# Rotary embedding on one core: the two head rows loaded as two transfers, one ahead of cosine, one behind sine

## The chip, the cores and the metric

The kernel runs on one core of one Trainium2 chip. The metric is the device time of one execution in microseconds (us). The kernel before took 316.34 us, the median of 3 runs (316.33 to 316.51).

## What is computed

The input x has 8 batches of 2048 positions, 16 heads and 64 values per head, in float32. Each head's 64 values are taken as two halves, which are rotated by the angle of their position:

```python
x1 = x[..., :32]; x2 = x[..., 32:]
cos = cos[None, :, None, :]; sin = sin[None, :, None, :]
out1 = x1 * cos - x2 * sin
out2 = x1 * sin + x2 * cos
return concatenate([out1, out2], axis=-1)
```

x and the output have 67.1 MB each; cosine and sine have 2048 x 32 values each, 256 KB.

## The kernel before

**Tiling.** Of a batch's 2048 positions each of the 128 partitions holds 16 consecutive ones (J = 16), called rows here. A row is 16 heads of 64 values (W = 1024 values, 4 KB in float32), and over all partitions one row of a batch is 512 KB. Work in SBUF is in 16-bit floats: `buf` has five slots of one batch each (SLOTS = 5), and batch b lives in slot b mod 5.

**Queues.** Nearly all of x goes through POOL's DMA queue, q0 in the profile, which turns float32 into float16 on the way in and back on the way out. The helper `queue` (lines 56 to 66) fixes the order in which these transfers are issued to the order of the calls in the program; I call it the ring. Two helpers issue on it: `load` (line 72) and `store` (line 75). Their records all stand at line 57. ScalarE's queue (q10) and SyncE's queue (q1) carry plain float32 transfers: sine on SyncE's (line 50), and cosine and then the head on ScalarE's (lines 51 and 52).

**The head.** The first two rows of batch 0 (JA = 2) do not come through the ring. They are loaded as float32 into `head` (line 44), which is the space of the first rows of slot 4 seen as 32-bit words, and ScalarE narrows them into slot 0 with `narrow_head` (line 95, the copy is line 96), first row 0 (JF = 1) and then row 1. The other 14 rows of batch 0 are the first load of the ring, load(0), at line 100. Since slot 4 holds the head until ScalarE has read it, load(3,2), the load of batches 3 and 4, has to wait for both `narrow_head` calls.

**Tables.** ScalarE also narrows the tables: sine twice into `sin_h` (line 101, and with the sign turned at line 102), and cosine once into `cos_h` (line 103). ScalarE runs its instructions in the order of the program.

**Rotation.** `rotate` (line 78) makes three VectorE instructions for some rows of one batch: the product of the swapped halves with sine into `v` (line 87), the product with cosine in place (line 91), and their sum in place (line 93).

**Order of the work.** The program's tail calls, in this order: load(0); the table copies and the two narrowings; rotate row 0 of batch 0; store of row 0 (512 KB of output); load(1,2), that is batches 1 and 2; load(3,2); rotate rows 1 to 15 of batch 0 and store them; rotate 1 and 2, and store both; and so on to batch 7. The last two rows of batch 7 are widened by ScalarE (line 127) and go out on SyncE's queue (line 128) when the first nine rows of batch 7 have been written.

So the order of the ring is: load(0), store of row 0, load(1,2), load(3,2), store of rows 1 to 15, store(1,2), load(5), load(6,2), store(3,2), store(5,2), and two stores of batch 7. POOL issues each of them only when what it needs is there, and those behind it wait on POOL.

Of the kernel before, what the change touches and what calls it, by code (L numbers as in the profile page):

```python
# [1 line left out]

# [4 lines left out]


@with_exitstack  # L10
def kernel(
    ctx: ExitStack,
    tc: tile.TileContext,
    x: bass.AP,
    cos: bass.AP,
    sin: bass.AP,
    out: bass.AP,
):
    nc = tc.nc
    f16 = mybir.dt.float16  # L20
    f32 = mybir.dt.float32

    B, S, H, D = x.shape
    Dh = D // 2
    P = nc.NUM_PARTITIONS
    J = S // P
    SLOTS = 5
    JA = 2
    JE = 2
    JF = 1  # L30

    pool = ctx.enter_context(tc.tile_pool(name="rope", bufs=1))
    buf = pool.tile([P, SLOTS, J, H, D], f16)
    v = pool.tile([P, J, H, D], f16)
    sin_f = pool.tile([P, J, Dh], f32)
    cos_f = pool.tile([P, J, Dh], f32)
    cos_h = pool.tile([P, J, Dh], f16)
    sin_h = pool.tile([P, J, D], f16)

    def words(slot, rows):  # L40
        flat = buf[:, slot, 0 : 2 * rows].rearrange("p j h d -> p (j h d)")
        return flat.bitcast(f32)

    head = words(SLOTS - 1, JA)
    tail = words(SLOTS - 2, JE)
    rows_in = x.rearrange("b (p j) h d -> p b (j h d)", j=J)
    rows_out = out.rearrange("b (p j) h d -> p b (j h d)", j=J)
    W = H * D

    nc.sync.dma_start(out=sin_f, in_=sin.rearrange("(p j) d -> p j d", j=J))  # L50
    nc.scalar.dma_start(out=cos_f, in_=cos.rearrange("(p j) d -> p j d", j=J))  # L51
    nc.scalar.dma_start(out=head, in_=rows_in[:, 0, 0 : JA * W])

    ring = []

    def queue(dst, src):
        dma = nc.gpsimd.dma_start(out=dst, in_=src)  # L57
        if ring:
            tc.add_manual_dep(
                dma.ins,  # L60
                ring[-1].ins.name,
                mybir.DependencyInfo(mybir.DependencyClass.NoSync, mybir.DependencyReason.DATA),
                reason="order of the ring",
            )
        ring.append(dma)
        return dma

    def part(b, n, j0, j1):
        s = b % SLOTS
        return buf[:, s : s + n, j0:j1].rearrange("p n j h d -> p n (j h d)")  # L70

    def load(b, n=1, j0=0):
        return queue(part(b, n, j0, J), rows_in[:, b : b + n, j0 * W : J * W])

    def store(b, n=1, j0=0, j1=J):
        return queue(rows_out[:, b : b + n, j0 * W : j1 * W], part(b, n, j0, j1))

    def rotate(b, j0=0, j1=J):
        n = j1 - j0
        js = slice(j0, j1)  # L80
        xt = buf[:, b % SLOTS, js]
        vt = v[:, js]
        shape = [P, n, H, 2, Dh]
        sin_b = sin_h[:, js, :].rearrange("p j (e d) -> p j e d", e=2).unsqueeze(2).to_broadcast(shape)
        cos_b = cos_h[:, js, :].unsqueeze(2).to_broadcast([P, n, 2 * H, Dh])
        xe = xt.rearrange("p j h (e d) -> p j h e d", e=2)
        nc.vector.tensor_mul(  # L87
            out=vt.rearrange("p j h (e d) -> p j h e d", e=2), in0=xe[:, :, :, ::-1, :], in1=sin_b
        )
        xw = xt.rearrange("p j h (e d) -> p j (h e) d", d=Dh)  # L90
        nc.vector.tensor_mul(out=xw, in0=xw, in1=cos_b)  # L91
        xa = xt.rearrange("p j h d -> p (j h d)")
        nc.vector.tensor_add(out=xa, in0=xa, in1=vt.rearrange("p j h d -> p (j h d)"))  # L93

    def narrow_head(j0, j1):
        nc.scalar.copy(  # L96
            out=buf[:, 0, j0:j1].rearrange("p j h d -> p (j h d)"), in_=head[:, j0 * W : j1 * W]
        )

    load(0, j0=JA)  # L100
    nc.scalar.copy(out=sin_h[:, :, Dh:D], in_=sin_f)  # L101
    nc.scalar.mul(out=sin_h[:, :, 0:Dh], in_=sin_f, mul=-1.0)  # L102
    nc.scalar.copy(out=cos_h, in_=cos_f)  # L103
    narrow_head(0, JF)
    narrow_head(JF, JA)
    rotate(0, 0, JF)
    store(0, j1=JF)
    load(1, 2)
    load(3, 2)
    rotate(0, JF, J)  # L110
    store(0, j0=JF)
    rotate(1)
    rotate(2)
    store(1, 2)
    load(5)
    load(6, 2)
    rotate(3)
    rotate(4)
    store(3, 2)
    rotate(5)  # L120
    rotate(6)
    store(5, 2)
    rotate(7)
    gate = store(7, j1=9)
    store(7, j0=9, j1=J - JE)

    nc.scalar.copy(out=tail, in_=buf[:, (B - 1) % SLOTS, J - JE : J].rearrange("p j h d -> p (j h d)"))  # L127
    end = nc.sync.dma_start(out=rows_out[:, B - 1, (J - JE) * W : J * W], in_=tail)
    tc.add_manual_dep(
        end.ins,  # L130
        gate.ins.name,
        mybir.DependencyInfo(mybir.DependencyClass.Sync, mybir.DependencyReason.DATA),
        reason="the last rows go out behind this part",
    )


# [1 line left out]
_INS = ['x', 'cos', 'sin']  # L138
_OUTS = [((8, 2048, 16, 64), 'float32')]


# [23 lines left out]
```

## Time and profile before

One execution was profiled. Its own time is 316.32 us, and its span from the first to the last instruction is 314.6 us.

| What | Value |
|---|---|
| Median of 3 runs | 316.34 us |
| Profiled execution / its span | 316.32 us / 314.6 us |
| VectorE busy, 27 instructions | 209.1 us |
| ScalarE busy, 7 instructions | 6.8 us |
| POOL's DMA queue q0, share of the 16 DMA engines | 98.1% |
| SyncE's queue q1 / ScalarE's queue q10 | 1.2% / 1.0% |
| HBM read and written | 67.63 MB and 67.11 MB |
| Issue to landing: sine / cosine / head | 3.7 / 3.9 / 12.1 us |
| Issue to landing: load(0) / store of row 0 | 22.6 / 8.4 us |

How to read the profile: DVE is VectorE, ACT is ScalarE, POOL is GpSimd and SP is SyncE. A line such as "L91 DVE TENSOR_TENSOR buf<-buf,cos_h" is an instruction of program line 91 that writes `buf` from `buf` and `cos_h`; what stands in brackets behind it is how long its engine was idle before it and what ended the wait. Line 57 stands for every transfer of the ring. The view by stretches gives, for each stretch of the span, the busy time of each engine and what share of the 16 DMA engines was busy with packets; a packet is counted with its whole length in the stretch where it starts, so short stretches can show shares over one, and long ones can be over or under by a little. A transfer is cut into packets: each of the 16 engines gets eight data packets of a 128-partition transfer and one small one that reports the completion.

### The profile page before, as it was taken

The numbers are of one execution on the slowest core, as the hardware profiler recorded it, in microseconds if no ns is written. First come the engines' busy times: TensorE is split into PE (matmuls) and PEld (weight loads), VectorE is DVE, ScalarE is ACT, GpSimd is POOL, SyncE is SP. The second block draws the span as 40 slices with busy tenths as digits, with TensorE's granted clock in tenths as the row PEclk, the third lists the DMA queues.
The fourth block names the chain that finished last, engine by engine and source line by source line (L and its number), as shares of the span: only waits on it lengthen the run. The fifth ranks groups of instructions, "written<-read, shape, count | busy, mean of one in ns | idle before, by whom it ended". The sixth has DMA issues, their size and how long they took to land.

```text
span 314.6 us, 113 instructions
## 1 busy us (share of the span) xinstructions
DVE 209.1 (66%) x27; ACT 6.8 (2%) x7; POOL 7.9 (3%) x16
## 2 busy tenths in 40 slices
DVE  0109991089999999999994399903999999200000
ACT  3200000000000000000000000000000000200000
POOL 1020000000000000000000000000000000100000
DMA  7989999999999899999999999999999999999998
GB/s 230 261 193 249 267 200 200 200 267 200 200 200 325 375 500 400 400 400 533 400 200 221 246 200 200 250 217 333 400 517 417 400 400 525 408 400 400 433 425 342
DMA packets 3072, 101.71 MB, mean 323 GB/s; under 512 B 256, under 2 KB 256, under 8 KB 640
## 3 DMA queue, kind: packets, MB, share of 16 engines
q0 software_dynamic: 2496, 99.09, 98.1%
q1 hardware_dynamic: 288, 1.31, 1.2%
q10 hardware_dynamic: 288, 1.31, 1.0%
HBM read 67.63 MB, written 67.11 MB: 428 GB/s over the span
## 4 chain that ended last, share of the span: by engine, by line
DVE 59%; DMA 19%; another core or an unknown queue 7%; ACT 1%; issue 0%; POOL 0%; ACTq 0%; DVEq 0%
DVE v L87 20%; DVE buf L91 20%; DVE buf L93 20%; DMA buf<-in_x_dram 19%; ACT buf L127 1%; ACT buf L96 0%; POOL out_dram L57 0%; ACTq L51 0%; DVEq L87 0%
## 5 line engine op out<-in xcount | busy, mean ns | idle before, releaser
L87 DVE TENSOR_TENSOR v<-buf,sin_h 128x16384 f16<-128x16384 f16 (+2 forms) x9 | 69.7, 7744 | 59.7 <-DMA buf<-in_x_dram 45.3
L91 DVE TENSOR_TENSOR buf<-buf,cos_h 128x16384 f16<-128x16384 f16 (+2 forms) x9 | 69.7, 7744 | 0.3
L93 DVE TENSOR_TENSOR buf<-buf,v 128x16384 f16<-128x16384 f16 (+2 forms) x9 | 69.7, 7744 | 0.3
L57 POOL DMA_DIRECT2D out_dram<-buf x7 | 4.3, 620 | 219.7 <-DVE buf L93 219.7
L127 ACT CAST buf<-buf 128x2048 f32<-128x2048 f16 x1 | 1.9, 1897 | 254.2 <-DVE buf L93 254.2
L57 POOL DMA_DIRECT2D buf<-in_x_dram x5 | 3.4, 679 | 43.0 <-DMA out_dram<-buf 42.2
L96 ACT CAST buf<-buf 128x1024 f16<-128x1024 f32 x2 | 2.0, 1042 | 7.2 <-DMA buf<-in_x_dram 7.2
L101 ACT ACT_TABLE_LOAD x1 | 1.3, 1283 | 1.7 <-PEq L149 1.7
L101 ACT CAST sin_h<-sin_f 128x512 f16<-128x512 f32 x1 | 0.6, 617 | 1.5 <-DMA sin_f<-in_sin_dram 1.5
L102 ACT ACTIVATE sin_h<-sin_f 128x512 f16<-128x512 f32 x1 | 0.6, 624 | 0.0
L103 ACT CAST cos_h<-cos_f 128x512 f16<-128x512 f32 x1 | 0.6, 601 | 0.0
L149 POOL MEMSET const-float32-0.0<- 128x1 f32 x1 | 0.1, 99 | 0.2 <-issue 0.2
L149 POOL MEMSET const-bfloat16-1.0<- 128x1 bf16 x1 | 0.1, 102 | 0.0
L149 POOL MEMSET const-float32-1.0<- 128x1 f32 x1 | 0.1, 99 | 0.0
L149 POOL MEMSET const-uint8-127<- 128x1 uint8 x1 | 0.1, 99 | 0.0
## 6 DMA issues: line engine op xcount, KB each, us to landing
buf<-in_x_dram POOLq DMA_DIRECT2D x3, 8192.0 KB, 57.1
out_dram<-buf POOLq DMA_DIRECT2D x1, 7680.0 KB, 71.7
out_dram<-buf POOLq DMA_DIRECT2D x1, 4608.0 KB, 35.5
buf<-in_x_dram POOLq DMA_DIRECT2D x1, 4096.0 KB, 57.3
buf<-in_x_dram POOLq DMA_DIRECT2D x1, 3584.0 KB, 22.6
out_dram<-buf POOLq DMA_DIRECT2D x1, 2560.0 KB, 41.0
buf<-in_x_dram ACTq DMA_DIRECT2D x1, 1024.0 KB, 12.1
out_dram<-buf SPq DMA_DIRECT2D x1, 1024.0 KB, 8.4
```

The lines of the kernel that those rows point to most:

```text
L57: dma = nc.gpsimd.dma_start(out=dst, in_=src)
L87: nc.vector.tensor_mul(out=vt.rearrange("p j h (e d) -> p j h e d", e=2), in0=xe[:, :, :, ::-1, :], in1=sin_b)
L91: nc.vector.tensor_mul(out=xw, in0=xw, in1=cos_b)
L93: nc.vector.tensor_add(out=xa, in0=xa, in1=vt.rearrange("p j h d -> p (j h d)"))
L96: nc.scalar.copy(out=buf[:, 0, j0:j1].rearrange("p j h d -> p (j h d)"), in_=head[:, j0 * W : j1 * W])
L101: nc.scalar.copy(out=sin_h[:, :, Dh:D], in_=sin_f)
L102: nc.scalar.mul(out=sin_h[:, :, 0:Dh], in_=sin_f, mul=-1.0)
L103: nc.scalar.copy(out=cos_h, in_=cos_f)
L127: nc.scalar.copy(out=tail, in_=buf[:, (B - 1) % SLOTS, J - JE : J].rearrange("p j h d -> p (j h d)"))
L149: nc = _bacc.Bacc("TRN2", target_bir_lowering=False, num_devices=1)
```

## The change

Three lines at the top and one in the order of the narrowings are touched.

```diff
     nc.sync.dma_start(out=sin_f, in_=sin.rearrange("(p j) d -> p j d", j=J))
+    nc.scalar.dma_start(out=head[:, 0:W], in_=rows_in[:, 0, 0:W])
+    nc.sync.dma_start(out=head[:, W : JA * W], in_=rows_in[:, 0, W : JA * W])
     nc.scalar.dma_start(out=cos_f, in_=cos.rearrange("(p j) d -> p j d", j=J))
-    nc.scalar.dma_start(out=head, in_=rows_in[:, 0, 0 : JA * W])
...
     nc.scalar.copy(out=sin_h[:, :, Dh:D], in_=sin_f)
     nc.scalar.mul(out=sin_h[:, :, 0:Dh], in_=sin_f, mul=-1.0)
+    narrow_head(0, JF)
     nc.scalar.copy(out=cos_h, in_=cos_f)
-    narrow_head(0, JF)
     narrow_head(JF, JA)
```

The head's one transfer of 1 MB becomes two of 512 KB. ScalarE's queue carries row 0 and then cosine; SyncE's queue carries sine and then row 1. On ScalarE the narrowing of row 0 goes ahead of that of cosine. The ring, the rotations and the stores are the same.

## The prediction

> **What bounds the kernel now.** I read the page first. VectorE is busy 66% of the span and the three other engines hardly at all, but the slices of the DMA engines stay at 8 or 9 tenths, and POOL's queue alone fills them.
>
> ```profile
> span 314.6 us, 113 instructions
> DVE 209.1 (66%) x27; ACT 6.8 (2%) x7; POOL 7.9 (3%) x16
> DMA  7989999999999899999999999999999999999998
> q0 software_dynamic: 2496, 99.09, 98.1%
> ```
>
> The slices are coarse, so I then cut the span into stretches at the points where POOL's transfers end (columns: stretch, length, busy times of DVE, ACT and POOL, PE clock, share of the 16 DMA engines, GB/s).
>
> ```profile
> 2.60:23.24 20.64, 2.07 (x3) 3.98 (x6) 1.95 (x3) 1.00 1.01 252
> 23.24:24.46 1.22, 0.52 (x1) 0.00 (x0) 0.00 (x0) 1.00 1.22 416
> 24.46:63.11 38.65, 23.95 (x3) 0.00 (x0) 0.55 (x1) 1.00 1.01 217
> 101.74:119.83 18.09, 18.02 (x3) 0.00 (x0) 0.71 (x1) 1.00 1.02 435
> 158.44:310.55 152.11, 88.24 (x11) 1.90 (x1) 3.25 (x5) 1.00 1.01 352
> ```
>
> In every stretch the share is one or a little over (a packet is counted where it starts): from about 2.6 us to the last transfer there is no gap on the engines. I checked this in the trace's packet records, where each packet of an engine starts as the one before ends. So the chain of waits, which names VectorE with 59%, misleads: VectorE's waits are for loads that stand in a full queue. The time is the start until the engines run (2.6), their work, and what follows the last packet. A change can matter in three ways only: another start, more or less packet time, or a **gap** in POOL's queue. The place for a gap is 23.24 us. There load(0) ends, and the store of row 0 and load(1,2) must already be asked for. This is the chain that asks for them:
>
> ```profile
> 4.45 0.62 ACT L101 CAST sin_h<-sin_f 128x512 f16<-128x512 f32 x1 [1.52 <-DMA sin_f<-in_sin_dram]
> 5.51 0.60 ACT L103 CAST cos_h<-cos_f 128x512 f16<-128x512 f32 x1
> 13.26 1.99 ACT L96 CAST buf<-buf 128x1024 f16<-128x1024 f32 x2 [7.15 <-DMA buf<-in_x_dram]
> 14.34 0.69 DVE L87 TENSOR_TENSOR v<-buf,sin_h 128x1024 f16<-128x1024 f16 x1 [14.34 <-ACT buf L96]
> 15.06 0.69 DVE L91 TENSOR_TENSOR buf<-buf,cos_h 128x1024 f16<-128x1024 f16 x1
> 15.79 0.69 DVE L93 TENSOR_TENSOR buf<-buf,v 128x1024 f16<-128x1024 f16 x1
> 16.79 0.53 POOL L57 DMA_DIRECT2D out_dram<-buf  x1 [14.88 <-DVE buf L93]
> ```
>
> The head rows land at 13.24, the store is issued at 16.79, and its first packet starts at 23.26 on the fastest engine, directly behind load(0). So 6.5 us lie between issue and need. How many of them are needed? At 116.42 a store of two batches is issued, and its packets (the last line below) start 3.45 us later, right behind the transfer before:
>
> ```profile
> 116.40:117.55 1.15, 1.15 (x1) 0.00 (x0) 0.71 (x1) 1.00 0.00 0
> 117.88:119.86 1.98, 1.98 (x1) 0.00 (x0) 0.00 (x0) 1.00 0.01 0
> 119.86:120.18 0.32, 0.32 (x1) 0.00 (x0) 0.00 (x0) 1.00 7.70 3277
> ```
>
> So issue to first packet is **at most 3.45 us**. At least it is the 0.53 of the issuing instruction. I call it the lead time and keep both ends.
>
> **How the queues share an engine.** Head packets after load(0) has started:
>
> ```profile
> 5.70:5.97 0.27, 0.00 (x0) 0.27 (x1) 0.00 (x0) 1.00 7.89 1699
> 7.80:8.10 0.30, 0.00 (x0) 0.00 (x0) 0.00 (x0) 1.00 1.07 437
> 8.12:8.42 0.30, 0.00 (x0) 0.00 (x0) 0.00 (x0) 1.00 7.07 1524
> 10.24:10.54 0.30, 0.00 (x0) 0.00 (x0) 0.00 (x0) 1.00 1.07 437
> ```
>
> 437 GB/s in 0.30 us are 131 KB, that is one 8 KB head packet on each of 16 engines; 1699 in 0.27 are 459 KB, one 28 KB packet of load(0) on each. They take turns, one packet each. A load packet takes 2.11 us, so the last two of eight head packets, which alone need 0.6 us, and the completion behind them (12.68) end at 12.95 in place of about 6.6. By the records SyncE's and ScalarE's queues take turns in the same way, 2 KB packets (sin, cos) 0.080 us apart; 8 KB packets are 0.306 apart. A line through both gives 0.155 for 4 KB.
>
> The Trainium skill, "DMA: Bandwidth & Descriptors", section "Queues, rings and completion order", says that an engine goes round robin between queues at packet granularity. The four rows above agree. The last transfer does not: by the timeline SyncE issues it at 305.26, and by the records its first packets run at 310.56, when POOL's queue has run out.
>
> **The change part by part.**
>
> Issues: ScalarE still issues two transfers (0.73 and 1.15); SyncE gets a second, at about 1.13. No ScalarE work is due before 4.45. Cost 0, and they hide behind the start.
>
> Packet time: eight 8 KB packets per engine (8 x 0.306 = 2.448) become sixteen of 4 KB (16 x 0.155 = 2.485), plus one completion packet (0.01 to 0.02), plus some four more changes between queues at 0.013 (head packets took 0.322 between load packets, 0.309 otherwise). Sum +0.1 us, on engines that never idle, so it is paid in full.
>
> Order at the start: this is the real edit. Before, sin and cos went first. After, sin shares with row 0, and cos, **second** on ScalarE's queue, shares with row 1. On the slowest engine the first head packet starts at 4.12, behind 16 small packets: 4.12 - 16 x 0.080 - 0.01 = 2.83 is its start. Eight pairs of 2 KB and 4 KB take 8 x 0.235 = 1.88; SyncE's queue is one packet ahead (0.155), completions 0.02: row 0 is done at 4.89, sin earlier. From there pairs of cos and row 1 run until load(0) comes in. Its first packet stood behind the sixth head packet on all engines, which began at 5.652 on the slowest and ended at 5.71 on the fastest: it became ready between these. (5.68 - 4.89)/0.235 = 3.4, so four cos packets pass and **four are left**, at 5.83. Each then costs a round of 2.11 + 0.235 = 2.35: 15.2, and one load packet more before the completion: 17.3. ScalarE started 0.3 after the slowest completion before, so cos is seen at 17.6, not at 4.4.
>
> What that delays: row 0 is seen at about 5.2 and sin near 5.0, ScalarE narrows sin (two times 0.53) and row 0 (1.05) by 7.2, and L87 runs then. But L91 needs cos: 17.6, cast 0.60 and 0.03, L91 to L93 0.73, L93 0.70, then 0.30 to the issue: 19.96, **3.2 us later than now**. The need is at 23.26 + 0.07 = 23.3. The lead time left is 3.37; at most 3.45 is wanted, at least 0.53. I take no gap: 0.08 us is the worst. load(1,2) follows 0.52 later and is wanted 1.2 later. Row 1 lands with cos at the latest, is narrowed by 19.3, and is wanted at 23.87 when load(0) is seen. load(3,2), which overwrites the head slot, is wanted at 63. So the earlier row 0 has nothing to win: even a store asked for at 9 us would stand behind load(0).
>
> Sum against the profiled execution's 316.32: +0.1, so 316.4; it stands 0.02 under the median of 316.34, which changes nothing.
>
> The page has a rule against the change: "Bandwidth" gives a fit of 2.0 us fixed plus bytes/436e3 per DMA and asks for 1 MiB or more. By it one transfer of 1 MiB (4.4) becomes two of 3.2, and the estimate is 318.4. In the records nothing of such a fixed part occupies an engine between cos and head.
>
> **Rivals.**
>
> *Cos is caught earlier, and a gap opens at 23.3 (slower).* For: of the 3.4 pairs only 0.4 is margin; if an engine has one more descriptor already taken when load(0) comes, or packets of 4 KB from x start less smoothly, five or six remain. Each more costs 2.35. Five: the store is issued at 22.3, and the gap is 22.3 + lead time - 23.3, 0 to 2.5 with the ends 0.53 and 3.45, so 316.4 to 318.9. Six: 24.7, gap 1.9 to 4.8, up to 321.2. It decides from an issue later than 19.9 to 22.8. Against: the same turns reproduce the head's 12.95.
>
> *Row 1 starves on SyncE's queue (slower).* For: the wait from 305.26 to 310.56. Then its last packets wait until load(1,2) ends at 63.1; narrowed at 65.1; load(3,2) is issued then (gap 2 to 5), rotation of row 1 to 15 starts there and not at 23.94, and two batches later store(1,2) at 142.4 comes some 18 to 21 after POOL's queue ran out: about 340. Against: ScalarE's queue was served in turn.
>
> *A fixed part per transfer (slower).* sin takes 3.7 us to landing with 0.64 of packets; if engines paid the other 3.1 once more: 319.5. Against: no such hole in the shares. The rule above is this case.
>
> *The start is quicker (faster).* Some engines end their first packet at 1.95 and get the next at 2.54. If x's packets fill that, up to 0.6 is won, and a little more with the slower first reads: 315.7.
>
> *The change does not do what it says:* SyncE's second transfer starts late, cos runs alone at 0.080 and lands before load(0). Also 316.4.
>
> **How the numbers follow.** About 0.2% (0.63 us) can be told from no change. Forecast 0.50; caught cos 0.33, of which 0.05 within 0.2%; starved row 0.07; fixed part 0.03; quicker start 0.04; doing nothing 0.03. Same 0.50 + 0.03 + 0.05 = 0.58, slower 0.28 + 0.07 + 0.03 = 0.38, faster 0.04. The range starts at 316.0 (run spread and a part of the quicker start) and reaches into the six-packet case with a middling lead time, 24.7 + 2.2 - 23.3 = 3.6, to 320.0.
>
> **What would show it.** Right: the cos cast near 17.6 and behind row 0's, the store issued near 20, load(0) ended near 23.3 with store packets directly behind, load(1,2) landed near 63.8. Wrong: shares under one around 23 to 28 us (caught cos), row 1's cast near 64 (starved), engines busy before 2.5 (quicker start). What would break it most easily is the count of four.

## The result and the profile after

The changed kernel takes 319.23 us (median of 4 runs, 319.2 to 319.4) against 316.34 (316.33 to 316.51): ratio 1.0091, 95% interval 1.0078 to 1.0103. It is **slower by 2.9 us** in these runs, which is 0.9%; a second set of runs below gave 1.7 us. The predicted 316.4 missed it, the range of 316.0 to 320.0 holds it, and what happened is the first of the rivals: cosine is caught by load(0), and POOL's queue runs short at 23 us.

The page of the changed kernel (span; slices of the DMA engines; share of POOL's queue):

```profile
span 317.4 us, 116 instructions
DMA  7989999999999999999999999999999999999997
q0 software_dynamic: 2496, 99.09, 97.6%
```

The engines still look full, and again the slices are too coarse. The timeline of the start shows the new order. The program is one line longer, so the lines of rotate, the ring and the narrowings stand one higher than before:

```profile
5.11 0.62 ACT L102 CAST sin_h<-sin_f 128x512 f16<-128x512 f32 x1 [2.18 <-DMA sin_f<-in_sin_dram]
7.22 0.69 DVE L88 TENSOR_TENSOR v<-buf,sin_h 128x1024 f16<-128x1024 f16 x1 [7.22 <-ACT buf L97]
20.43 0.62 ACT L105 CAST cos_h<-cos_f 128x512 f16<-128x512 f32 x1 [13.24 <-DMA cos_f<-in_cos_dram]
21.08 0.69 DVE L92 TENSOR_TENSOR buf<-buf,cos_h 128x1024 f16<-128x1024 f16 x1 [13.16 <-ACT cos_h L105]
22.81 0.53 POOL L58 DMA_DIRECT2D out_dram<-buf  x1 [20.89 <-DVE buf L94]
23.33 1.44 POOL L58 DMA_DIRECT2D buf<-in_x_dram  x2
```

Row 0 is indeed early: its first product runs at 7.22 in place of 14.34. Then VectorE waits 13.16 us for cosine, which is seen at 20.43 and not at 4.4. The store of row 0 is issued at 22.81, 6.0 us later than before, and load(0) ends on the first engine at 23.47.

Where the 2.9 us are is read from the stretches between the ends of POOL's transfers, each taken on the engine that is first (columns as in the prediction). After:

```profile
2.60:23.47 20.87, 2.08 (x3) 3.98 (x6) 0.66 (x2) 1.00 1.01 244
23.47:25.11 1.64, 0.19 (x1) 0.00 (x0) 1.30 (x2) 1.00 0.87 297
25.11:64.49 39.38, 24.28 (x3) 0.00 (x0) 0.55 (x1) 1.00 1.01 214
64.49:103.80 39.31, 37.87 (x5) 0.00 (x0) 0.00 (x0) 1.00 1.01 213
103.80:121.89 18.09, 18.02 (x3) 0.00 (x0) 0.71 (x1) 1.00 1.02 435
121.89:312.62 190.73, 126.65 (x15) 1.90 (x1) 3.81 (x6) 1.00 1.01 368
312.62:316.24 3.62, 0.00 (x0) 0.00 (x0) 0.00 (x0) 1.00 0.72 295
```

And the stretches of before that the prediction did not show:

```profile
63.11:101.74 38.63, 37.80 (x5) 0.00 (x0) 0.00 (x0) 1.00 1.01 217
119.83:310.56 190.73, 126.71 (x15) 1.90 (x1) 3.82 (x6) 1.00 1.02 368
310.56:313.34 2.78, 0.00 (x0) 0.00 (x0) 0.00 (x0) 1.00 0.91 374
```

| Stretch | Before | After | Lost |
|---|---|---|---|
| start to the end of load(0) | 20.64 | 20.87 | 0.23 |
| store of row 0 | 1.22 | 1.64 | 0.42 |
| load(1,2) | 38.65 | 39.38 | 0.73 |
| load(3,2) | 38.63 | 39.31 | 0.68 |
| store of rows 1 to 15 | 18.09 | 18.09 | 0 |
| from 119.83 (before) or 121.89 (after) to SyncE's last transfer | 190.73 | 190.73 | 0 |
| from there to the last packet of the last engine | 2.78 | 3.62 | 0.84 |

The sum is 2.90; the two profiled executions differ by 319.21 - 316.32 = 2.89. Three things are to be seen. Everything behind 104 us runs at exactly the old pace. The store's stretch is the only one with a visible hole (share 0.87). And the last row is no wait at the end, but the spread of the 16 engines, the time from the first to the last of them to end a transfer. By the packet records it is 0.29 us before, from the end of load(0) to the end of the program. After, it is 0.99 at the end of load(0), 0.57 at the end of the store of row 0, 0.90 and 1.12 at the ends of the two loads, and 1.12 from there on. The program is done when its slowest engine is.

So what counts is the engine that is last, and by the packet records its account reads otherwise than the table, which follows the engine that is first. The last engine ends load(0) at 24.46 in place of 23.53, which loses 0.93. It takes 1.22 us for the store of row 0, as before, so the hole costs it nothing: the store's packets, which start at 23.91, are there before it is done with load(0). It takes 39.71 in place of 38.65 for load(1,2) and 39.54 in place of 38.63 for load(3,2), 1.06 and 0.91 lost. That is 0.93 for the start and 1.97 for the two loads behind the short queue, 2.90 in all.

The stretches of load(1,2) and load(3,2) show shares of 1.01 and hide their loss, because a packet that stands, that is, whose record is longer than that of others of its size, is counted as busy. The packet records show it. The first packet of load(1,2), which takes 2.43 us before, takes 2.60 to 3.43 on the 16 engines; so does the **last** packet of load(3,2), at 101 us, with 2.76 to 3.45. (A load of two batches has sixteen data packets on each engine; the eight named above hold for one batch.)

### The profile page after: what moved, and what is told of

Same layout as the page of the kernel before. It is cut to its first block, busy times and chain, and to the rows that moved or that the text cites. A ratio compares the mean times of both kernels' runs of the same rounds, so it can differ in the third digit from the quotient of the medians.

```text
span 317.4 us, 116 instructions
## 1 busy us (share of the span) xinstructions
DVE 209.1 (66%) x27; ACT 6.8 (2%) x7; POOL 7.9 (2%) x16
## 4 chain that ended last, share of the span: by engine, by line
DVE 58%; DMA 19%; another core or an unknown queue 7%; ACT 1%; issue 0%; POOL 0%; ACTq 0%; DVEq 0%
DVE buf L92 19%; DVE buf L94 19%; DVE v L88 19%; DMA buf<-in_x_dram 13%; DMA cos_f<-in_cos_dram 6%; ACT buf L128 1%; ACT cos_h L105 0%; POOL out_dram L58 0%; ACTq L51 0%; DVEq L88 0%
```

## The experiments

Two theories. **Short ring**: the store of row 0 and load(1,2) are asked for too late, POOL's queue runs short at 23 us, and that costs the hole and both standing packets; the expectations call this theory dry queue or late ring. **Start**: the new order of the first packets costs time and sets the engines apart, whatever the ring does. In each run the kernel before was timed on the same chip: medians 316.36 to 316.43.

**The changed kernel once more (a1).** No edit.

> The changed kernel once more, unchanged, for a second profile. Its first trace loses 0.93 us (last engine) by the end of load(0), 1.06 more by the end of load(1,2) and 0.91 more by the end of load(3,2), where all engines stand for about 0.7 us near 101 us. If all three belong to the kernel: 319.2 and the same three steps. If the third is a chance event of that one execution: 318.3 and no stand near 101 us.

Measured: 318.16 (317.08 to 318.49), ratio 1.0060 [1.0043, 1.0076]. So the changed program lies between 317.08 and 319.40 over both sets of runs, where the one before lies between 316.24 and 316.81 over all of them. The profiled execution was the quickest, 317.08:

```profile
18.15 0.62 ACT L105 CAST cos_h<-cos_f 128x512 f16<-128x512 f32 x1 [10.55 <-DMA cos_f<-in_cos_dram]
20.53 0.53 POOL L58 DMA_DIRECT2D out_dram<-buf  x1 [18.62 <-DVE buf L94]
24.47:63.12 38.65, 24.47 (x3) 0.00 (x0) 0.55 (x1) 1.00 1.02 221
63.12:101.74 38.62, 37.06 (x5) 0.00 (x0) 0.00 (x0) 1.00 1.01 217
```

Cosine came one round earlier, 18.15 against 20.43. The store was issued 2.7 us ahead of the end of load(0), and both load stretches are those of before. What is left is the spread of the engines, 1.03 us in place of 0.29: that is 0.74, and the execution is 317.08 - 316.32 = 0.76 slower than the profiled one of before. The execution profiled first was 2.13 slower than this one; by the two traces one round of load packets decides over two thirds of the loss. Neither outcome that I had written down fits: the three steps are not one fixed cost.

**A late store in the old kernel, first try (b1).**

```diff
+    for _ in range(8):
+        nc.vector.tensor_mul(out=..., in0=..., in1=...)
     rotate(0, 0, JF)
```

> The kernel before, with VectorE repeating the first product of row 0 eight more times (8 x 0.73 = 5.8 us of idle VectorE time), so that the store of row 0 is issued near 22.6 us as in the changed kernel, while the start of the queues stays as before. Dry queue theory (the loss comes from POOL's queue running out at 23.3): load(1,2) ends 1.0 to 1.2 us later, 317.4; 318.3 if the loss near 101 us follows from the dry queue too. Start theory (the loss comes from reading x beside sine at the start): 316.3, no loss.

Measured: 346.02, ratio 1.0937 [1.0921, 1.0954]. This missed its aim: with the added instructions the compiler's schedule put VectorE's work on rows 1 to 15 ahead of that on row 0, and the store of row 0 was issued at 50.14. It shows the price of an empty ring without any cover: in 23.30 to 52.40 the DMA share is 0.05, and of these 29.1 us the kernel lost 29.6.

**The same, second try (h6, h4, h2).** ScalarE repeats the narrowing of row 0; VectorE is held to its old order by a dependency without a wait.

```diff
-    narrow_head(0, JF)
+    for _ in range(7):        # h4: 5, h2: 3
+        narrow_head(0, JF)
```

> The kernel before, with ScalarE repeating the narrowing of row 0 six more times (6 x 0.95 = 5.7 us), and VectorE held to its order of before: the start of the queues stays as before, and the store of row 0 is issued near 22.5 us, as late as in the changed kernel's first profile (22.81). Late ring theory: the first packet of load(1,2) and the last of load(3,2) stand for 0.5 to 1.0 us each, 317.3 to 318.4. Start theory (those stands come from engines that the start has set apart): 316.4.

> The same with four more copies: the store issued near 21.9 us, 1.2 before load(0) ends. Late ring theory: hardly any gap before the store's packets (the lead time in the changed kernel was 1.1), but stands at the first packet of load(1,2) and the last of load(3,2): 317.2 to 318.4. Rival (only the time in which the queue is empty is lost): 316.4 to 316.6.

> The kernel before with the narrowing of row 0 repeated two more times; VectorE waits for all copies (1.04 each, four of them from 13.2, and 2.5 to the issue), so the store of row 0 is issued near 19.9 us, 3.3 before load(0) ends on the first engine. Late ring theory, with the changed kernel's second profile (issue at 20.53, no stand): 316.4. If the ring needs the 3.45 us that the trace of before could prove: a loss of 0.1 to 0.5.

| Run | Store issued | Ahead of the end of load(0) | Time | Ratio |
|---|---|---|---|---|
| h2 | 19.73 | 3.5 | 316.56 (316.31 to 318.33) | 1.0011 [0.9999, 1.0022] |
| h4 | 21.91 | 1.2 | 318.91 (317.74 to 320.02) | 1.0090 [1.0054, 1.0126] |
| h6 | 24.02 | -0.9 | 321.03 (319.54 to 322.03) | 1.0151 [1.0111, 1.0191] |

h6 was issued later than I had meant, since the repeats stood behind the narrowing of row 1 and VectorE waited for all of them. The stretches of h4 (store of row 0, load(1,2), load(3,2)):

```profile
23.11:24.33 1.22, 0.50 (x1) 0.00 (x0) 0.76 (x2) 1.00 1.11 379
24.33:63.44 39.11, 23.98 (x3) 0.00 (x0) 0.55 (x1) 1.00 1.01 216
63.44:103.16 39.72, 38.73 (x5) 0.00 (x0) 0.00 (x0) 1.00 1.01 211
```

The start is that of before, and the engines end load(0) within 0.41 us. The store's own stretch is the old 1.22, so there was no hole at all. Still load(1,2) loses 0.46 and load(3,2) 1.09. The late refill alone, with the start of before, makes both standing packets; the rival, that only the empty time is lost, falls. (Of h4's four runs two took 317.74 and 318.00, the profiled one, and two 319.83 and 320.02; what the slower pair lost on top is in no profile.) In h6 there is a hole as well:

```profile
23.13:26.33 3.20, 3.14 (x2) 0.00 (x0) 1.96 (x3) 1.00 0.47 163
26.33:65.77 39.44, 21.91 (x3) 0.00 (x0) 0.55 (x1) 1.00 1.01 213
65.77:105.29 39.52, 38.48 (x5) 0.00 (x0) 0.00 (x0) 1.00 1.01 212
```

Here 1.98 go into the hole, 0.79 and 0.89 into the two stands. An issue 3.5 us ahead costs nothing that most of h2's runs can tell (nine of ten took 316.31 to 316.63, one without a profile 318.33), 2.7 cost the loads nothing in a1's profile, and 1.2 cost them 0.46 + 1.09 = 1.55 in h4's (318.00; the median of its runs is higher).

**Only load(3,2) late (k1).** Why should its last packet stand, 77 us after it was asked for? Row 1's narrowing is repeated, so that the store and load(1,2) go out on time and load(3,2) alone is late; VectorE is held to its order as in h6.

```diff
-    narrow_head(JF, JA)
+    for _ in range(9):
+        narrow_head(JF, JA)
```

> The kernel before with the narrowing of row 1 repeated eight more times: the store of row 0 and load(1,2) are issued on time (near 17), only load(3,2), which waits for row 1's copies, is issued near 23.7, some 39 us before its packets are due. If the stand at the last packet of load(3,2) comes from its own late issue: 317.1 to 317.4 and a stand near 100 us. If it follows from POOL's queue having been short near 23: 316.4 and no stand.

Measured: 316.37 (316.30 to 316.68), ratio 1.0000 [0.9990, 1.0009].

```profile
16.55 0.53 POOL L57 DMA_DIRECT2D out_dram<-buf  x1 [14.63 <-DVE buf L93]
23.91 0.72 POOL L57 DMA_DIRECT2D buf<-in_x_dram  x1 [6.12 <-DMA buf<-in_x_dram]
63.11:101.74 38.63, 37.78 (x5) 0.00 (x0) 0.00 (x0) 1.00 1.01 217
```

Asked for at 23.91, as late as in the changed kernel (24.03), load(3,2) takes the old 38.63. So its stand is not made by its own late issue; it comes with a queue that was short when load(1,2) began. By the packet records all 16 engines have it in the changed kernel, b1, e1, h4 and h6, where the store was late; none has it before, in h2 and in k1, and three have it in a1, where the loss does not show on the first engine or on the last.

**A ring that cannot run short (c1, e2, i1, g1, c2).** load(1,2) is issued directly behind load(0), ahead of the store of row 0, and otherwise only the start, with ScalarE's order of work behind it, differs.

```diff
     load(0, j0=JA)
+    load(1, 2)
...
     store(0, j1=JF)
-    load(1, 2)
```

c1 is the changed kernel with this ring, c2 the kernel before with it. e2 has the tables first and the head in two transfers on two queues, i1 the same on ScalarE's queue alone, g1 the head whole and ahead of cosine.

> The changed kernel with load(1,2) issued right behind load(0), ahead of the store of row 0, so that POOL's queue cannot run out at 23.3 us although cosine still lands near 20. Dry queue theory: the two later steps of 1.06 and 0.91 are gone, and only what the start costs stays: 317.3 or less. Start theory: the loss stays, 318.3 to 319.2.

> The kernel before with load(1,2) issued behind load(0), ahead of the store of row 0; tables first, head in one transfer. First of four that all have this safe ring, so that only the start differs. Both theories: 316.4; if the order of the ring itself costs or wins, it shows here.

> Tables first, head in two transfers of 4 KB packets on two queues, load(1,2) ahead of the store of row 0. Late ring theory: what e1 lost at load(1,2) and load(3,2) is back, and what its start costs stays: 316.6 to 316.9. If 4 KB packets of x set the engines apart wherever they stand: near c1's 317.4.

> As the safe ring with tables first, but the head as two transfers of 4 KB packets on one queue: ScalarE asks for cosine, row 0, row 1. If the size of the packets sets the engines apart: near the 317.06 of e2. If it takes two queues that alternate: near the 316.50 of c2.

> ScalarE asks for the whole head in one transfer of 8 KB packets and then for cosine; cosine is narrowed last; load(1,2) ahead of the store of row 0. If reading x in the first packets of the program sets the engines apart: near c1's 317.4. If it takes 4 KB packets on two queues: near c2's 316.4.

| Run | First packets | Head | Time | Ratio |
|---|---|---|---|---|
| c2 | tables | one, 8 KB packets | 316.50 | 1.0004 [0.9995, 1.0014] |
| g1 | sine and x | one, 8 KB packets | 316.68 | 1.0009 [1.0000, 1.0019] |
| e2 | tables | two queues, 4 KB packets | 317.06 | 1.0019 [1.0010, 1.0028] |
| i1 | tables | one queue, 4 KB packets | 317.17 | 1.0027 [1.0016, 1.0038] |
| c1 | sine and x | two queues, 4 KB packets | 317.44 | 1.0033 [1.0020, 1.0046] |

The order of the ring costs nothing that c2's runs can tell; its trace has a small stand too, at the last packet of load(1,2), with 2.56 to 2.86 in place of 2.43, so that a stand is not peculiar to a short queue. The changed kernel with the safe ring still loses 1.0: this is the start's part. The split makes 0.56 of it with the tables first (e2 less c2) and 0.76 with x first (c1 less g1); reading x in the first packets makes 0.18 and 0.38, but there the intervals of the compared runs overlap, so that this part is not shown. i1 is with e2 and not with c2, so it is not the alternation of two queues but the split into two transfers of 4 KB packets; the size of the packets and the number of transfers were not tried apart. The runs of this table are from three chips (c1; c2, e2 and g1; i1). By the packet records the slowest engine ends load(0) at 24.09 in i1 and e2 and at 23.45 in c2 and g1. i1 holds a second answer:

```profile
6.19 1.04 ACT L97 CAST buf<-buf 128x1024 f16<-128x1024 f32 x1 [0.31 <-DMA buf<-in_x_dram]
9.71 0.57 POOL L58 DMA_DIRECT2D out_dram<-buf  x1 [7.08 <-DVE buf L94]
24.59 1.04 ACT L97 CAST buf<-buf 128x1024 f16<-128x1024 f32 x1 [17.36 <-DMA buf<-in_x_dram]
```

Here row 0 is early and cosine is on time, and the store is issued at 9.71. It wins nothing, but in this ring it stands behind load(1,2) in any case, so that i1 does not test what an early row 0 is worth in the old one.

**The split with the tables first and the old ring (e1).**

```diff
     nc.scalar.dma_start(out=cos_f, in_=...)
-    nc.scalar.dma_start(out=head, in_=rows_in[:, 0, 0 : JA * W])
+    nc.scalar.dma_start(out=head[:, 0:W], in_=rows_in[:, 0, 0:W])
+    nc.sync.dma_start(out=head[:, W : JA * W], in_=rows_in[:, 0, W : JA * W])
```

> The head as two transfers, but behind the tables: ScalarE asks for cosine and then row 0, SyncE for sine and then row 1; ScalarE narrows in the order of before. Dry queue theory: row 0 lands by about 15, the store is issued by 19, nothing runs out: 316.4. Start theory: the first packets are those of before: 316.4. If the split itself costs (more and smaller packets, a fixed part for each transfer): 316.6 to 319.5.

Measured: 318.13 (317.94 to 318.66), ratio 1.0058 [1.0043, 1.0073]. The time falls into the last of the three cases, but only in part for its reason, the split. Both rows were caught: they took turns with load(0), row 0 was seen at 17.99 (the whole head, before, at 13.24), and the store was issued at 21.52. That is 1.6 us ahead of the end of load(0), and by the packet records load(1,2) and load(3,2) lose 0.33 and 0.63 on the first engine, as in h4. e2, the same start with the safe ring, is 1.07 faster; the other 0.6 is what the split costs in e2. So the short ring comes with a late store whatever made it late.

## Why the prediction was right or wrong, step by step

*What bounds the kernel: right.* The DMA engines set the time, and the only dangerous place was 23 us. That an early row 0 wins nothing is argued from the order of the ring and not shown: in the changed kernel row 0's first product ran at 7.22, but the next one had to wait for cosine.

*The order at the start: the mechanism was right, the count was wrong.* The step that failed is "four are left". By the packet records five cosine packets were left in the changed kernel on 9 of the 16 engines when load(0) came in, four on six and two on one. That is 4.4 in the mean, so the forecast was near for the mean engine; but it took one count for all of them, and the slowest decides. Their load(0) started between 5.64 and 7.17, where before it was 5.71 to 5.96. Cosine was seen at 20.43 and not at 17.6; in a1, where four were left at most, at 18.15. I had written that only 0.4 of a pair was margin; with rounds of 2.35 us that was no ground for a forecast of the good side. The expectation for e1 made the same error again. The taking of turns itself, which the Trainium skill states ("DMA: Bandwidth & Descriptors", section "Queues, rings and completion order"), is borne out: cosine moved by 2.28 us from one execution to the other (20.43 and 18.15), near one round of 2.35.

*The lead time: the bounds held, but they bound the wrong thing.* Issue to the first packet was 1.10 (22.81 to 23.91 by the packet records), inside 0.53 to 3.45. But it is not all that the queue wants: h4 was issued 1.2 ahead, had no hole, and lost 1.55 in two packets that stood. The 3.45 that the trace of before showed to be enough was the better number to plan with.

*The price of the rival: too low.* With an issue at 22.81 and 1.10 of lead time its formula gives a gap of 0.6 and a time of 317.0. Measured on the first engine were 0.42 in the store's stretch, 0.73 and 0.68 in the two loads, 1.83 in all; on the last engine the store's stretch lost nothing and the two loads 1.97. So the gap that the formula prices was not what cost the time, and the stands were in none of my cases. The range was drawn for this rival, but that its real price fits in is luck: the range reached to 320.0 for six packets left and a gap of 3.6, and neither happened.

*Packet time: mis-sized.* I had +0.1 on every engine. The split costs 0.56 to 0.76 (the runs with the safe ring), because the engines come apart and the last one counts: in the profiles of e2 and c2 the first engine ends the program's last transfer at about the same time (313.02 and 313.08), the last one at 314.06 and 313.40. In the changed kernel's profile the first engine ends load(0) 0.23 later than before and the last one 0.93. The sum had no term for the difference between the engines. The Trainium skill's fit of 2.0 us for each DMA ("DMA: Bandwidth & Descriptors"; it stands in its section "Anatomy of one DMA", for transfers from POOL, and not in "Bandwidth", as the prediction has it) had the right sign against the split; the measured 0.56 to 0.76 lie between the 2.0 that it adds for one more transfer, an estimate, and my 0.1.

*The other rivals.* Row 1 did not starve for good: in the changed kernel it was narrowed at 20.95, right behind cosine. But in i1, second on ScalarE's queue, it was caught with all its packets and seen at 24.59, when load(0) was over. A fixed part for each transfer of 2 to 3 us is not there; i1 and e2 have two transfers for one and lose 0.6 and 0.8 against the kernel before. The start was not quicker.

What stays open: why the last packet of load(3,2) stands when the queue was short 75 us earlier (k1 excludes its own issue time, h4 excludes the spread of the engines), and why 4 KB packets set the engines apart. For both I have only where and how much. For the second the records say where: in e2 16 of the head's 256 packets took 0.22 to 0.36 us in place of the usual 0.16, and in c2 none of the 128 packets of 8 KB took over 0.32 in place of 0.31. Nor was it tried apart whether the store or load(1,2) must not be late: load(1,2) was issued 1.8 us ahead of its first packet in the changed kernel, 1.9 in h4 and 2.3 in e1, where this packet stood (in e1 on seven engines), and 3.5 in a1, where it did not. Only two executions of the changed kernel have a profile, so that the round in which cosine lands explains the other ones too is likely and not shown. No kernel here beats the one before.

## What to carry to other kernels

A small transfer that is not through when a stream of big packets starts pays one big packet for each of its own: count, for each engine and not for the mean one, what will be left then of everything that the critical chain needs, and put in front what this chain cannot do without. Where one DMA queue sets the time, its next work has to be asked for some time before it runs out (here 2.7 us were enough in one profile and 1.2 were not); a hole that is just closed was already too late. And look at the slowest of the 16 engines: a mean share of one hides both a packet that stands and engines that come apart.

## What the runs showed of the hardware

- In h4 the queue was refilled 1.2 us before it ran out and shows no hole, and two packets stand nevertheless: the first of the next load (0.3 us in the mean of the 16 engines) and the last of the load behind that (1.1). In the changed kernel, refilled 0.7 us before the first engine ran out, these are 0.7 and 0.7.
- A stand of this kind is seen in no share of busy time; the length of the stretch (39.72 in place of 38.63) and the packet's own record show it.
- From the end of load(3,2) on, near 102 us, the spread of the 16 engines stays the same within 0.01 us to the end of the program in every trace (0.29 before, 1.12 in the changed kernel, 1.03 in a1). Ahead of that it can move: from 0.50 to 0.32 over load(1,2) in c2, and from 0.99 to 0.57 in the changed kernel where the queue ran short.
- Splitting a 1 MB load of x into two of 512 KB costs 0.6 to 0.8 us here, on one queue or on two. By the packet records the head's packets take 0.2 us more in the mean of the engines (43.30 us over all 16 in e2, 39.97 in c2), and the spread of the engines at the end of load(0) grows from 0.50 to 0.94.
